# Attention stage of a hybrid decoder block: sink columns a unit ahead, background steps behind the unit's own, the gated result cast a unit later

## The chip, the cores and the metric

The kernel runs on one NeuronCore of a Trainium2 chip. The metric is the device time of one launch in microseconds (us). Lower is better.

The engines of the core are named as in the profile: PE is the matrix engine (TensorE), with PEld its loads of weights; DVE is the vector engine; ACT the scalar engine; POOL is GpSimd; SP is the engine that issues nearly all the DMAs here. A trailing q (SPq, DVEq) is the sequencer of that engine.

## The reference, cut to what matters

The block has 1024 positions of 1024 channels. It normalises the input, makes one wide projection of it, runs sliding-window attention (16 heads of 64, 4 key heads, window 128, one learned sink logit per head) beside a gated linear recurrence, gates both, projects both, merges them, projects once more and normalises.

```python
q, k, v, g_attn, xr, g_rnn, m_attn, m_rnn = jnp.split(h @ w_in[l], SPLIT_POINTS, axis=-1)
...
m = jnp.maximum(jnp.max(s, axis=-1, keepdims=True), sink)      # s: masked scores of 128 queries
p = jnp.exp(s - m)                                             #    against 256 keys
denom = jnp.sum(p, axis=-1, keepdims=True) + jnp.exp(sink - m)
o = jnp.einsum('bnkgqs,bnskd->bnqkgd', p / denom, vb)
...
y_attn = o * jax.nn.silu(g_attn)
merged = (jax.nn.sigmoid(m_attn) * (y_attn @ w_attn_proj[l])
          + jax.nn.sigmoid(m_rnn) * (y_rnn @ w_rnn_proj[l]))
x = x + gate[:, None, :] * (merged @ w_out[l])
```

Everything is float32. A large product is made of three products of a rounded part ("hi", ACT casts it) and a rest ("lo", DVE subtracts it): hi x hi, lo x hi, hi x lo.

## The kernel before

**The stages.** Up to about 575 us the kernel makes the projections (lines 200 to 850). From about 583 to 778 us it runs attention together with background matmuls. After that it projects the attention result (`ap_k`, line 1412), merges, and makes the output projection (line 1468 on) up to 964 us. The change lies wholly in the attention stage.

**A unit.** Attention is cut into 32 units of one key head group g = u // 8 and one block of 128 queries n = u % 8, four heads at once. The loop is at line 1331 and runs 35 turns, because a unit's steps lie up to three turns apart. From line 360 on the instruction order on PE, ACT, DVE, POOL and SP is the order in which the program calls them (`manual_schedule`, line 361): each engine does its instructions in that order, and an instruction that waits holds up all behind it on its engine. In turn u:

- `scores(u)` (997): 8 matmuls into the tile `s_ps`, of which there is one buffer. It also takes a tile `p` (`px`, three buffers) of 4 heads x 129 columns, and POOL copies the sink logits into column 129 (line 1012). In odd turns it issues loads of keys and queries (`load_kq`).
- `maxima_a(u)` (1017): ACT copies half of the scores into `px`. `maxima_d(u)` (1021): DVE copies the other half where the window's mask says so (1025; in units with n = 0 POOL's `affine_select` masks instead, 1028), and reduces `px`, sink column included, to the maxima (1030).
- `weights_a(u-1)` (1032): four exponentials on ACT. `weights_d(u-1)` (1038): DVE takes the reciprocal of the sums (1041) and multiplies (1042).
- `values(u-3)` (1071): 4 matmuls into `pv` (2 where n = 0), one buffer; at even units it issues loads of values (`load_v`).
- `join_a(u-3)` (1085): two ACT copies out of `pv` into `ob`. `join_d(u-3)` (1092): two DVE additions into `yq` (1099, 1100).
- `transposed(u-2)` (1045): four PE transposes of the weights into `pt`, one buffer.
- `split_a(u-2)` (1052): ACT casts `pt` to `phc`. `split_d(u-2)` (1057): DVE subtracts to `plc` (1060), and POOL masks both to `phm` and `plm` (1065; not where n = 0). `values` of the next turn needs all four.

**What runs between.** `piece()` (1325) advances a generator by one background product of 12 matmuls: for six turns the last slots of the projection (`run`, 623), after that the products of `rp_steps` (1132), tile `rp`. One turn has one piece, the 34th has two. A piece also calls small background steps: `prep_r` (1110) casts a half of a weight chunk on ACT and makes its rest on DVE (line 104, tile `wl`), in two of four turns; `finish` (1146) copies a finished accumulator on ACT (1150, tile `rp`) and stores it, once in four turns. They go through `put` (457), which calls them on the spot, so they stand in the engines' order ahead of `weights_d`, `join` and `split` of that turn. Stores are put off to `flush()` (594), after the pieces.

**The gated result.** Every second turn `a_prep(m)` (1195) handles two finished units: f1 multiplies `yq` by the gate on DVE (1202), f2 casts it on ACT (1207, tile `ah`), f3 subtracts the rest on DVE (1212 or 1217, tile `al`). f1 and f2 are called in one turn between `weights_d` and `values`, f3 at the same place one turn later.

Of the kernel before, what the change touches and what calls it, by code (L numbers as in the profile page):

```python
# [12 lines left out]
F32 = mybir.dt.float32  # L13
# [9 lines left out]
P = 128  # L23
S = 1024
D = 1024
# [24 lines left out]
def tile_hybrid_block(ctx, tc, x, pk, rows, posr, posi, invf, c_row, w_ss, w_gate, w_main, w_v,  # L50
                      w_g, w_ap, w_rp, w_out, out):
    nc = tc.nc
    V, A, G, T = nc.vector, nc.scalar, nc.gpsimd, nc.tensor
# [5 lines left out]
    def f32(ap):  # L59
        return ap.bitcast(F32)  # L60
# [41 lines left out]
    def rest(dst, src, scale=1.0):  # L102
        if scale == 1.0:
            V.tensor_tensor(out=dst[1][:], in0=src, in1=f32(dst[0][:]), op=ALU.subtract)  # L104
        else:
            V.scalar_tensor_tensor(out=dst[1][:], in0=src, scalar=scale, in1=f32(dst[0][:]),  # L106
                                   op0=ALU.mult, op1=ALU.subtract)
# [285 lines left out]
    W = {}  # L393
# [63 lines left out]
    def put(st_):  # L457
        Load.act = max(Load.act, Load.pe) + st_[1]
        Load.dve = max(Load.dve, Load.pe) + st_[2]
        st_[3]()  # L460
# [133 lines left out]
    def flush():  # L594
        while behind:
            behind.pop(0)()
# [121 lines left out]
    gq = []  # L718
# [244 lines left out]
    at = psx = None  # L963
    U = {}
# [12 lines left out]
    def load_kq(m):  # L977
        g, t0 = m // 4, (m % 4) * 256
        ks = at.tile([P, 2, 384], F32R, tag="ks", name="ks", bufs=2)
        kv = k_d.rearrange("(b a r j) t -> j (a r) b t", b=2, a=2, r=32, j=4)[g]  # L980
        lo = P if t0 == 0 else 0
        for rep in range(2):
            dma(ks[rep * 64:(rep + 1) * 64, :, lo:], kv[:, :, t0 - P + lo:t0 + 256])
        qs = at.tile([P, 4, 256], F32R, tag="qs", name="qs", bufs=2)
        dma(qs[:], q_d[g].rearrange("(a j) t -> a j t", j=4)[:, :, t0:t0 + 256])
        U["kq", m] = ks, qs

    def load_v(m):
# [5 lines left out]
        dma(vs[:, lo:, :], vs_d[g][:, n0 - 1 + lo:n0 + 1, :])  # L994
        U["v", m] = vs, dv

    def scores(u):
        g, n = u // 8, u % 8
        ks, qs = U["kq", u // 2]
        qc = slice((n % 2) * P, (n % 2 + 1) * P)  # L1000
        k0 = (n % 2) * P
        s_full = psx.tile([P, 1024], F32, tag="s", name="s_ps")
        s_ps = s_full[:].rearrange("p (j k) -> p j k", j=4)
        for j in range(4):
            o = s_ps[:, j, :] if n else s_ps[:, j, P:]
            for b in range(2):
                W["pe"] = T.matmul(o, qs[:, j, qc], ks[:, b, k0 + (0 if n else P):k0 + 256],  # L1007
                                   start=(b == 0), stop=(b == 1))
        px = at.tile([P, 4, P + 1], F32, tag="p", name="p", bufs=3)
        sm = at.tile([P, 2, 4], F32, tag="small", name="small", bufs=4)  # L1010
        gs = slice(g * 4, (g + 1) * 4)
        G.tensor_copy(px[:, :, P:P + 1], W["sink"][:, gs].unsqueeze(2))
        U["s", u] = s_ps, px, sm
        if n % 2 and u // 2 + 2 < 16:
            load_kq(u // 2 + 2)

# [40 lines left out]
    def split_d(u):  # L1057
        pt, phc = U.pop(("t", u))
        plc = at.tile([P, 4, P], F32R, tag="plc", name="plc")
        V.tensor_tensor(out=plc[:], in0=pt[:], in1=f32(phc[:]), op=ALU.subtract)  # L1060
        ms = []
        if u % 8:
            for s_, tag in ((phc, "phm"), (plc, "plm")):
                d_ = at.tile([P, 4, P], F32R, tag=tag, name=tag)
                G.affine_select(out=d_[:], in_=f32(s_[:]), pattern=[[0, 4], [1, P]],
                                compare_op=ALU.is_ge, fill=0.0, base=0,
                                channel_multiplier=-1)
                ms.append(d_)
        U["m", u] = [phc, plc], ms
# [34 lines left out]
    rp_acc, R, O = [], {}, {}  # L1104

    def load_r(e):
        src = w_rp[e] if e < KC else w_ap[e - KC]
        R[e] = [load_half(src[:, SL[i]]) for i in range(2)]

    def prep_r(e, i):  # L1110
        def f1():
            O[e, i] = slot()
            cast(O[e, i], R[e][i])
        put(("A", 0.62, 0, f1))
        put(("D", 0, 0.69, lambda: rest(O[e, i], R[e][i])))

    def load_y(c):
        if c < 2:
# [13 lines left out]
    def rp_steps():  # L1132
        h_ctx.close()
        pb_ctx.close()
        psr = pool(ctx, "psr", space=PSUM, side="right")
        rp_acc.extend(psr.tile([P, S], F32, name=f"rp{i}") for i in range(2))
        W["yp"] = pool(ctx, "ypool", bufs=12)
        W["tout"] = pool(ctx, "tout", bufs=1)
        W["hpool"] = pool(ctx, "hpool", bufs=7)

        def part(c, kc2):
            for kc in (2 * kc2, 2 * kc2 + 1):
                W["pe"] = mm_k([rp_acc[c % 2][:, t] for t in SL], (O.get((c, 0)), O.get((c, 1))),
                               kc, xh=yh, xl=yl)

        def finish(c):
            def f():
                flush()
                t = W["tout"].tile([P, S], F32, tag="rp", name="rp32")
                A.copy(t[:], rp_acc[c % 2][:])  # L1150
                store(tr_d[c], t[:])
            put(("A", 1.1, 0, f))

        seq = [(c, k) for k in range(4) for c in range(2)]
        seq += [(c, k) for c in range(2, KC) for k in range(4)]
        load_y(2)
        load_y(3)
        for i, (c, k) in enumerate(seq):
            part(c, k)
            if i in (1, 2, 3, 4):  # L1160
                load_y(i + 3)
            if i in (1, 2):
                prep_r(i - 1, 1)
            if i in (6, 10):
                finish(0 if i == 6 else 1)
            if i >= 8 and k == 1 and c > 2:
                finish(c - 1)
            if i % 4 == 2:
                load_r((i + 2) // 4 + 1)
            if i >= 4 and i % 4 < 2:  # L1170
                prep_r((i + 4) // 4, i % 4)
            yield
        finish(7)
# [21 lines left out]
    def a_prep(m):  # L1195

        g, t0 = m // 4, (m % 4) * 256
        y = U.pop(("yq", m))

        def f1():  # L1200
            gq = U.pop(("gq", m))
            V.tensor_tensor(out=y[:], in0=y[:], in1=gq, op=ALU.mult)

        def f2():
            if not AH:
                a_alloc()
            A.copy(U["ah", g][:, :, t0:t0 + 256], y[:])

        def f3():
            h = f32(U["ah", g][:, :, t0:t0 + 256])  # L1210
            if g < 3:
                V.tensor_tensor(out=U["al", g][:, :, t0:t0 + 256], in0=y[:], in1=h,
                                op=ALU.subtract)
            else:
                for a in range(2):
                    o = AL[g][a][t0 // HALF][:, t0 % HALF:t0 % HALF + 256]
                    V.tensor_tensor(out=o, in0=y[:, a, :], in1=h[:, a, :], op=ALU.subtract)

        return [[("D", 0, 0.69, f1), ("A", 0.62, 0, f2)], [("D", 0, 0.8, f3)]]


    C_GA, C_XR, C_GR, C_MA, C_MR = 10, 18, 26, 34, 42
# [102 lines left out]
    def piece():  # L1325
        nonlocal left
        left -= 1
        next(more)

    late, low, loaded = [], [], {}  # L1330
    for u in range(32 + 3):
        todo = (left - KEEP + (35 - u) // 2) // (35 - u)
        if u < 32:
            scores(u)
            maxima_a(u)
            maxima_d(u)
        if 1 <= u < 33:
            weights_a(u - 1)
        for _ in range(todo - todo // 2):
            piece()  # L1340
        flush()
        if 1 <= u < 33:
            weights_d(u - 1)
        for st_ in low:
            put(st_)
        low = []
        if "hpool" in W and late and ("gq", late[0]) in U and u >= loaded[late[0]] + 2:
            first_, low = a_prep(late.pop(0))
            if late:
                first_, low = first_ + low, []  # L1350
            for st_ in first_:
                put(st_)
        if u >= 3:
            values(u - 3)
            join_a(u - 3)
            join_d(u - 3)
        if 2 <= u < 34:
            transposed(u - 2)
            split_a(u - 2)
            split_d(u - 2)  # L1360
        for _ in range(todo // 2):
            piece()
        if u >= 3 and u % 2 == 0:
            late.append((u - 3) // 2)
        if u >= 2 and len(loaded) < 16 and len(loaded) <= (u - 2) // 2 and (
                len(loaded) - (late[0] if late else (u - 2) // 2) < 2):
            m = len(loaded)
            load_gq(m)
            loaded[m] = u
    del W["att"]  # L1370
    for st_ in low + [st_ for m in late for group in a_prep(m) for st_ in group]:
        put(st_)
    flush()
    at_ctx.close()
    psx_ctx.close()
# [8 lines left out]
    hpool, ypool = W["hpool"], W["yp"]  # L1384
# [223 lines left out]
```

## Time and profile before

| What | Value |
|---|---|
| median of 3 runs | 969.53 us (969.5 to 971.67) |
| the profiled execution's own time | 965.91 us |
| its span, first to last instruction | 963.9 us |
| busy share of the span: PE, DVE, ACT, POOL | 96%, 71%, 55%, 8% |
| granted TensorE clock, mean | 0.999 of full |
| scores of the first unit start | 582.88 us |
| scores of the last unit start | 753.31 us |
| last matmul of `values` starts | 776.72 us |

The profile is of one execution, and all times of its rows are from the span's start. Busy PE counts matmuls that overlap: a 128x512 matmul is shown with 0.39 us, but the next one starts 0.23 us later. So PE's busy share says little about how much time a stage could lose, and the starts of the same step in successive turns say more. In rows of the timeline the columns are the start, the duration, the engine, the line, the operation, out<-in, the shape, the count, and in brackets the idle time of the engine before it with what ended that.

### The profile page before, as it was taken

Reading aid. Unit: us, or ns where it says so; the run is one execution under the profiler, and the core shown is the slowest. Engines: PE = TensorE matmul, PEld = TensorE weight load, DVE = VectorE, ACT = ScalarE, POOL = GpSimd, SP = SyncE. Lnnn points to the kernel's source line nnn. Section 1 sums busy time; section 2 is a strip of 40 time slices with the busy share of each in tenths; the row PEclk is TensorE's granted clock in tenths of the full one; section 3 lists DMA queues with packets and bytes.
Section 4 is the critical chain, followed back from the end, with each engine's and each line's share of the span. In section 5 each row is a group of like instructions: output and inputs, shape, how many; then the busy total and the mean of one; then the engine's idle time right before and its main releaser. Section 6 shows DMA issues by size and latency. Waiting matters only on the chain.

```text
span 963.9 us, 12413 instructions
## 1 busy us (share of the span) xinstructions
PE 922.8 (96%) x4261; PEld 746.6 (77%) x4261; DVE 685.0 (71%) x1068; ACT 530.6 (55%) x1036; POOL 81.2 (8%) x137
## 2 busy tenths in 40 slices
PE   5899999999999999999999989989999999999997
PEld 3688687778888888888888768767777788888886
DVE  8978798767659946875796787777878736655532
ACT  7435645454567665956675776767776622212311
POOL 1055000000000000000000001123232200000000
PEclk9999999999999999999999999999999999999999
DMA  8824575751333532353233349896655285536321
GB/s 322 345 66 165 205 268 191 254 186 45 110 109 109 190 106 89 125 181 109 91 139 132 142 151 302 265 333 195 194 164 178 66 305 179 173 129 219 128 90 65
DMA packets 84275, 164.19 MB, mean 170 GB/s; under 512 B 12771, under 2 KB 33251, under 8 KB 84214
## 3 DMA queue, kind: packets, MB, share of 16 engines
q1 hardware_dynamic: 83350, 161.09, 48.9%
q0 software_dynamic: 720, 2.07, 0.6%
q8 instruction: 33, 0.54, 0.2%
q14 instruction: 28, 0.23, 0.1%
q10 hardware_dynamic: 144, 0.26, 0.1%
HBM read 114.00 MB, written 49.78 MB: 170 GB/s over the span
## 4 chain that ended last, share of the span: by engine, by line
PE 67%; DVE 7%; ACT 6%; DMA 5%; issue 4%; POOL 1%; SPq 0%; DVEq 0%; ACTq 0%; POOLq 0%
PE bk L502 36%; PE rp L165 9%; PE pmain L165 5%; PE rp L1473 5%; PE pgate L775 5%; PE pmain L1473 4%; DMA ks<-k_d 2%; PE pv L1079 1%; PE s_ps L1007 1%; DVE wl L104 1%; DMA dv<-dv_d 1%; DMA r<-w_rp 1%; ACT wh L98 1%; DVE plc L1060 1%; ACT p L1035 1%
## 5 line engine op out<-in xcount | busy, mean ns | idle before, releaser
L502 PE MATMUL bk<-nh,wl 128*128 128x512 f32 x368 | 143.9, 391 | 1.9 <-DVE wl L104 1.7
L502 PE MATMUL bk<-nl,wh 128*128 128x512 f32 x368 | 144.4, 392 | 0.0
L502 PE MATMUL bk<-nh,wh 128*128 128x512 f32 x368 | 144.4, 392 | 0.0
L104 DVE TENSOR_TENSOR wl<-r,wh 128x512 fp32r<-128x512 f32 x108 | 74.4, 693 | 18.9 <-ACT wh L98 18.8
L98 ACT CAST wh<-r 128x512 fp32r<-128x512 f32 x108 | 66.3, 618 | 37.0 <-PE pmain L165 10.0
L502 PEld LDWEIGHTS bk<-nh,wl 128*128 128x128 f32 x368 | 69.1, 188 | 18.8 <-DVE wl L104 3.0
L502 PEld LDWEIGHTS bk<-nl,wh 128*128 128x128 f32 x368 | 69.1, 188 | 15.2
L502 PEld LDWEIGHTS bk<-nh,wh 128*128 128x128 f32 x368 | 69.1, 188 | 14.3
L502 PE MATMUL bk<-hh,wl 128*128 128x512 f32 x184 | 71.9, 391 | 0.9 <-DVE wl L106 0.5
L502 PE MATMUL bk<-hl,wh 128*128 128x512 f32 x184 | 72.2, 392 | 0.0
L502 PE MATMUL bk<-hh,wh 128*128 128x512 f32 x184 | 72.2, 392 | 0.0
L104 DVE TENSOR_TENSOR wl<-ws,wh 128x512 fp32r<-128x512 f32 x80 | 54.2, 683 | 4.3 <-ACT wh L98 4.3
L98 ACT CAST wh<-ws 128x512 fp32r<-128x512 f32 x80 | 48.2, 615 | 4.0 <-DVE ws L524 2.2
L1035 ACT ACTIVATE p<-p,small 128x129 f32<-128x129 f32 x128 | 50.0, 400 | 0.0
L502 PEld LDWEIGHTS bk<-hh,wl 128*128 128x128 f32 x184 | 34.5, 188 | 9.5 <-DVE wl L104 0.9
L502 PEld LDWEIGHTS bk<-hl,wh 128*128 128x128 f32 x184 | 34.6, 188 | 7.6
L502 PE MATMUL bk<-hha,wl 128*128 128x512 f32 x92 | 36.5, 397 | 4.0 <-DVE wl L104 3.9
L502 PEld LDWEIGHTS bk<-hh,wh 128*128 128x128 f32 x184 | 34.6, 188 | 7.2
L1007 PE MATMUL s_ps<-ks,qs 128*128 128x256 f32 (+1 forms) x256 | 37.6, 289 | 0.0
L605 ACT ACTIVATE c<-bk 128x512 f32<-128x512 f32 x31 | 18.5, 596 | 33.6 <-PE bk L502 31.4
L502 PE MATMUL bk<-hha,wh 128*128 128x512 f32 x92 | 36.2, 394 | 0.0
L502 PE MATMUL bk<-hla,wh 128*128 128x512 f32 x92 | 36.1, 392 | 0.0
(339 smaller groups left out, 2184.9 us busy)
## 6 DMA issues: line engine op xcount, KB each, us to landing
r<-w_main SPq DMA_DIRECT2D x100, 256.0 KB, 4.1
wada<-w_ss SPq DMA_DIRECT2D x16, 512.0 KB, 8.4
qs<-q_d SPq DMA_DIRECT2D x16, 512.0 KB, 6.0
ks<-k_d SPq DMA_DIRECT2D x24, 192.0 KB, 4.4
xt<-x SPq DMA_DIRECT2D x8, 512.0 KB, 7.4
q_d<-rhi SPq DMA_DIRECT2D x16, 256.0 KB, 3.9
q_d<-rlo SPq DMA_DIRECT2D x16, 256.0 KB, 3.6
wg<-w_gate SPq DMA_DIRECT2D x8, 512.0 KB, 4.7
```

What stands on the lines that cost most here:

```text
L98: A.copy(dst[0][:], src)
L104: V.tensor_tensor(out=dst[1][:], in0=src, in1=f32(dst[0][:]), op=ALU.subtract)
L165: mm = T.matmul(ps[hf], ww, xx[kc][hf], start=(kc == 0 and ww is w_h and xx is xh), stop=(kc == KC - 1 and xx is xl))
L502: W["pe"] = T.matmul(ps, ww[:, c], b[kc][xx_], start=(first and kc == 0 and i == 0), stop=(kc == 3 and i == 2), skip_group_check=not first)
L605: A.activation(t["t"], s(), AF.Tanh, scale=0.5)
L775: W["pe"] = T.matmul(ps[:, SL[hf]], ww[:, c0:c0 + P], xx_[:, SL[hf]], start=(ic == 0 and i == 0), stop=(ic == 1 and i == 2))
L1007: W["pe"] = T.matmul(o, qs[:, j, qc], ks[:, b, k0 + (0 if n else P):k0 + 256], start=(b == 0), stop=(b == 1))
L1035: A.activation(px[:, j, :], px[:, j, :], AF.Exp, bias=sm[:, 0, j:j + 1], accum_out=sm[:, 1, j:j + 1])
L1060: V.tensor_tensor(out=plc[:], in0=pt[:], in1=f32(phc[:]), op=ALU.subtract)
L1079: W["pe"] = T.matmul(pv[:], b, m[:].rearrange("p j q -> p (j q)"), start=(i == 0), stop=(i == len(prods) - 1))
L1473: T.matmul(ps[:, sl], lhs[k][th][:, ts_], w[:, sl], start=(k == 0 and w is h_ and lhs is mh), stop=(k == KC - 1 and lhs is ml))
```

## The change

- A new step `sink(u)` takes the tile `px` and lets POOL write the sink column. It is called for unit u+1 in turn u, after `split` and ahead of the masks; `scores` takes the tile from there.
- The masks on POOL become a step of their own (`masks`), called behind `split_d` and `sink`.
- `prep_r` and `finish` no longer call their ACT and DVE steps on the spot: they append them to two lists, and `do_later()` calls all ACT steps, then all DVE steps, at the end of the turn. Outside the attention loop they are called at once, as before.
- `a_prep` returns its three steps. In the loop f1 is called at the end of a turn, f2 in the next turn behind `weights_a` and ahead of the pieces, f3 at the end of that turn.
- All pieces of a turn are called ahead of `values`. This differs in the one turn with two pieces.

```diff
+    def sink(u):
+        px = U["p", u] = at.tile([P, 4, P + 1], F32, tag="p", name="p", bufs=3)
+        gs = slice(u // 8 * 4, u // 8 * 4 + 4)
+        G.tensor_copy(px[:, :, P:P + 1], W["sink"][:, gs].unsqueeze(2))
+
     def scores(u):
...
-        px = at.tile([P, 4, P + 1], F32, tag="p", name="p", bufs=3)
         sm = at.tile([P, 2, 4], F32, tag="small", name="small", bufs=4)
-        gs = slice(g * 4, (g + 1) * 4)
-        G.tensor_copy(px[:, :, P:P + 1], W["sink"][:, gs].unsqueeze(2))
-        U["s", u] = s_ps, px, sm
+        U["s", u] = s_ps, U.pop(("p", u)), sm
...
         V.tensor_tensor(out=plc[:], in0=pt[:], in1=f32(phc[:]), op=ALU.subtract)
+        U["m", u] = phc, plc
+
+    def masks(u):
+        phc, plc = U["m", u]
         ms = []
...
+    later_a, later_d = [], []
+
     def prep_r(e, i):
         def f1():
             O[e, i] = slot()
             cast(O[e, i], R[e][i])
-        put(("A", 0.62, 0, f1))
-        put(("D", 0, 0.69, lambda: rest(O[e, i], R[e][i])))
+        later_a.append(f1)
+        later_d.append(lambda: rest(O[e, i], R[e][i]))
+        if "att" not in W:
+            do_later()
+
+    def do_later():
+        for todo in (later_a, later_d):
+            while todo:
+                todo.pop(0)()
...
                 A.copy(t[:], rp_acc[c % 2][:])
                 store(tr_d[c], t[:])
-            put(("A", 1.1, 0, f))
+            later_a.append(f)
+            if "att" not in W:
+                do_later()
...
-        return [[("D", 0, 0.69, f1), ("A", 0.62, 0, f2)], [("D", 0, 0.8, f3)]]
+        return f1, f2, f3
...
-    late, low, loaded = [], [], {}
+    late, high, loaded = [], [], {}
+    sink(0)
     for u in range(32 + 3):
...
         if 1 <= u < 33:
             weights_a(u - 1)
-        for _ in range(todo - todo // 2):
+        low = [steps_[2] for steps_ in high]
+        while high:
+            high.pop(0)[1]()
+        for _ in range(todo):
             piece()
         flush()
         if 1 <= u < 33:
             weights_d(u - 1)
-        for st_ in low:
-            put(st_)
-        low = []
-        if "hpool" in W and late and ("gq", late[0]) in U and u >= loaded[late[0]] + 2:
-            first_, low = a_prep(late.pop(0))
-            if late:
-                first_, low = first_ + low, []
-            for st_ in first_:
-                put(st_)
         if u >= 3:
             values(u - 3)
...
             split_d(u - 2)
-        for _ in range(todo // 2):
-            piece()
+        if u + 1 < 32:
+            sink(u + 1)
+        if 2 <= u < 34:
+            masks(u - 2)
+        if "hpool" in W:
+            for f in low:
+                f()
+            if late and ("gq", late[0]) in U and u >= loaded[late[0]] + 2:
+                high.append(a_prep(late.pop(0)))
+                high[0][0]()
+        do_later()
         if u >= 3 and u % 2 == 0:
             late.append((u - 3) // 2)
```

After the loop what is left of `high` and `late` is called in the order f1, f2, f3, as before.

More of the change, by code (lines that the diff above doesn't have):

```diff
@@ L1370, in tile_hybrid_block @@
     del W["att"]
-    for st_ in low + [st_ for m in late for group in a_prep(m) for st_ in group]:
-        put(st_)
+    for steps_ in high:
+        steps_[1]()
+        steps_[2]()
+    for m in late:
+        for f in a_prep(m):
+            f()
     flush()
```

## Prediction

> **What bounds the kernel now.** I read the page first, then the stage by windows, then the chain of waits, the sum of waits and the timeline of single turns.
>
> ```profile
> span 963.9 us, 12413 instructions
> ```
>
> ```profile
> 616.00:652.00 36.00, 31.80 (x160) 23.78 (x159) 27.25 (x51) 24.79 (x81) 8.62 (x17) 1.00 1.02 317
> 660.00:760.00 100.00, 95.35 (x491) 74.21 (x490) 80.68 (x152) 74.24 (x237) 26.44 (x52) 1.00 0.49 155
> ```
>
> The columns of the windows are the stretch, its length, busy time of PE, PEld, DVE, ACT and POOL with their counts, the granted clock, the DMA share and GB/s. The attention stage has two halves. Up to 652 us the DMA engines are full (share 1.02). After 660 us they are half idle (0.49), DVE is busy for 81% and PE looks full at 95%, which for overlapping matmuls does not say that it lost nothing. The chain of waits has the same border:
>
> ```profile
> 620.15 8.64 DMA ks<-k_d
> 628.86 8.47 DMA r<-w_rp
> 637.34 8.70 DMA dv<-dv_d
> ...
> 697.60 0.95 PE s_ps L1007 x8
> 698.55 2.76 PE rp L165 x12
> 701.31 0.93 PE pv L1079 x4
> 702.25 0.44 PE pt L1049 x4
> ```
>
> From 620 to 646 us the end of one load starts the next. No order of ACT and DVE steps makes that shorter. The last four rows are one turn in which PE waits for nothing: 0.95 + 2.76 + 0.93 + 0.44 = 5.08 us. That is the least a turn can take. Now the turns as they are (start of scores, and for the turns without scores the first matmul of the piece):
>
> ```profile
> 652.33 1.19 PE L1007 MATMUL s_ps<-ks,qs 128*128 128x256 f32 x8
> ...
> 753.31 1.19 PE L1007 MATMUL s_ps<-ks,qs 128*128 128x256 f32 x8
> ...
> 758.98 0.71 PE L165 MATMUL rp<-yh,wh 128*128 128x512 f32 x2
> ...
> 765.59 0.71 PE L165 MATMUL rp<-yh,wh 128*128 128x512 f32 x2
> ```
>
> Turns 13 to 30 are 18 turns in 753.31 - 652.33 = 100.98 us. In two of them (units 16 and 24) `values` has 2 matmuls instead of 4, which makes 5.08 - 0.46 = 4.62. So the least is 16 x 5.08 + 2 x 4.62 = 90.5, and 10.5 us are lost. Turn 31 takes 758.98 - 753.31 = 5.67, lost 0.6. Turn 32 has no scores, least 5.08 - 0.95 = 4.13; it takes 765.59 - 758.98 = 6.61, lost 2.5. Together **13.6 us** that PE loses after the DMA half. The waits (window 652 to 776 us) and one bad turn show to what:
>
> ```profile
> ACT ah L1207 <- DVE yq L1202: 28.8, 11, 3.7
> DVE yq L1099 <- ACT ob L1089: 16.4, 11, 2.0
> PEld pv L1079 <- ACT phc L1054: 7.8, 7, 2.0
> ```
>
> ```profile
> 689.04 0.99 ACT L1150 COPY rp<-rp 128x1024 f32<-128x1024 f32 x1
> 690.25 1.20 PE L1007 MATMUL s_ps<-ks,qs 128*128 128x256 f32 x8
> 690.72 0.68 DVE L104 TENSOR_TENSOR wl<-r,wh 128x512 fp32r<-128x512 f32 x1
> 691.32 0.17 DVE L1041 RECIPROCAL small<-small 128x4 f32<-128x4 f32 x1
> 691.53 0.69 DVE L1042 TENSOR_TENSOR p<-p,small 128x512 f32<-128x512 f32 x1
> 692.14 0.69 DVE L1202 TENSOR_TENSOR yq<-yq,r 128x512 f32<-128x512 f32 x1
> 692.86 0.62 ACT L1207 CAST ah<-yq 128x512 fp32r<-128x512 f32 x1 [2.30 <-DVE yq L1202]
> 693.49 0.37 ACT L1088 COPY ob<-pv 64x256 f32<-64x256 f32 x1
> 694.25 0.59 ACT L1054 CAST phc<-pt 128x512 fp32r<-128x512 f32 x1
> 694.26 0.42 DVE L1099 TENSOR_TENSOR yq<-pv,ob 64x256 f32<-64x256 f32 x1 [1.44 <-ACT ob L1089]
> 694.69 0.43 DVE L1100 TENSOR_TENSOR yq<-pv,ob 64x256 f32<-64x256 f32 x1
> 694.74 0.59 ACT L1019 COPY p<-s_ps 128x512 f32<-128x512 f32 x1
> 695.15 0.69 DVE L1060 TENSOR_TENSOR plc<-pt,phc 128x512 fp32r<-128x512 f32 x1
> 695.22 0.42 ACT L1035 ACTIVATE p<-p,small 128x129 f32<-128x129 f32 x1
> 695.22 0.46 PE L1079 MATMUL pv<-phc,vs 128*128 128x512 f32 x1 [1.01 <-ACT phc L1054]
> 695.76 0.74 DVE L1025 COPY_PREDICATED p<-mgt,s_ps 128x512 f32<-128x512 uint32 x1
> 695.97 0.64 POOL L1065 TENSOR_SCALAR_AFFINE_SELECT plm<-plc 128x512 fp32r<-128x512 f32 x1 [0.36 <-DVE plc L1060]
> 696.39 0.39 ACT L1035 ACTIVATE p<-p,small 128x129 f32<-128x129 f32 x1
> 696.78 0.69 DVE L1030 TENSOR_REDUCE small<-p 128x4 f32<-128x516 f32 x1 [0.28 <-POOL p L1012]
> 697.36 1.19 PE L1007 MATMUL s_ps<-ks,qs 128*128 128x256 f32 x8
> ```
>
> This turn takes 697.36 - 690.25 = 7.11 us. ACT and DVE wait for each other in turn. ACT's `ah` cast stands ahead of `ob` and `phc` and waits 2.30 us for DVE's f1, which stands behind `wl`, the reciprocal and the multiplication. Then DVE idles 1.44 us for `ob`, and PE idles for `phc`. So the bound after 652 us is a loop of DVE and ACT, not PE. DVE's steps from start to start: `wl` 0.60, reciprocal 0.21, multiplication 0.61, f1 0.61, idle 1.44 or a little more, additions 0.43 + 0.46, `plc` 0.61, masked copy 0.74, idle 0.28, reduction 0.61: some 6.6 us against PE's 5.08.
>
> **The change part by part.**
>
> *The `ah` cast a turn later.* f1 runs at the end of a turn, f2 in the next turn behind the exponentials, over a microsecond after f1 ends. So ACT's 2.30 and DVE's 1.44 go. Without the two idles and without f1 or `wl` ahead of it, the loop is only DVE's own work: 0.21 + 0.61 + 0.43 + 0.46 + 0.61 + 0.74 + 0.61 = 3.67, plus one of f1 and f3 (0.61) each turn = 4.28, plus `wl` (0.60) in two of four turns = 4.88; mean 4.58. That is under 5.08, so PE's own 5.08 becomes the bound.
>
> *Background behind the unit's own.* I check the chain in a turn without stalls, time 0 at its scores. `values` ends at 0.95 + 2.76 + 0.93 = 4.64, the last matmul 0.16 later (0.39 shown, 0.23 apart): 4.8. The two `ob` take 694.25 - 693.49 = 0.76: 5.55. `phc` to 6.14. DVE adds from 5.55 to 6.44, `plc` to 7.13, POOL's `plm` starts 0.13 later (695.97 against 695.84) and ends at 7.9. PE wants `plm` for the fourth matmul of the next `values`, at 5.08 + 3.71 + 0.69 = 9.48. That is 1.6 us to spare, where now it is short. What is moved goes behind `plc`: f1 or f3 to 7.66, `wl` to 8.26. Who now waits for it is the masked copy of the next unit: it runs to 9.0, the reduction to 9.6, reciprocal and multiplication to 10.4, and the next additions are due at 5.55 + 5.08 = 10.63. The masked copy frees the only `s_ps`, which PE wants at 10.16: 1.1 to spare. ACT: `phc` to 6.14, a cast of weights 0.62, copy of scores 0.59, exponentials 696.78 - 695.22 = 1.56, `ah` 0.62, to 9.5; the next `ob` is due at 9.88. Once in four turns `finish` (0.99) comes in too, and ACT is then 0.6 late for `ob`; the 1.6 cover it. I leave 0.6 in all for the five or so turns where this comes together with `ah`. The weights so prepared are for products three turns later, so half a turn of delay costs nothing. `finish` reads an accumulator that is overwritten three pieces on: nothing either.
>
> *Sink a unit ahead.* It now waits on POOL for the transposes of the same turn (`px` has three buffers), at about 5.3, ahead of `phm`, which can start only after `phc` at 6.14; the copy is short enough for that gap. Queued behind it are only the masks. It saves DVE the 0.28 ahead of the reduction. These lie in the same loop and in the 13.6, not beside it. If the gap were gone, each mask would come 0.2 later, inside the 1.6.
>
> *Stores and loads on SP.* `finish` a half turn later means its store is flushed a turn later. Before, SP stood at it:
>
> ```profile
> SPq L57 <- ACT rp L1150: 42.9, 8, 13.7
> ```
>
> The loads of values behind it now go first. At a DMA share of 0.49 that is worth nothing to PE. In the DMA half no `finish` has come yet, and the bytes ahead of `dv` are the same, so 646 us stays.
>
> *Two pieces in one turn* ahead of `values`: in the next turn one piece then covers the chain to `plm`. As computed, that suffices: nothing.
>
> Where the port between DVE and POOL comes in, there is one row of each:
>
> ```profile
> 630.06 1.07 POOL L1065 TENSOR_SCALAR_AFFINE_SELECT phm<-phc 128x512 fp32r<-128x512 f32 x1 [1.56 <-ACT phc L1054]
> ...
> 630.55 1.12 DVE L1212 TENSOR_TENSOR al<-yq,ah 128x512 fp32r<-128x512 f32 x1
> ```
>
> A mask that takes 0.64 takes 1.07 here, and f3, which takes 0.69 like f1, takes 1.12, while they overlap: 0.43 for each. After the change f1 or f3 starts right behind `plc`, when `plm` starts too, so this meeting becomes the rule. If POOL loses, `plm` ends at 8.4 or, behind `wl` as well, 9.1: still in time. I take that end (DVE starts 0.1 to 0.2 earlier); the other end is the first rival. The Trainium skill, "SBUF — State Buffer", section "Who interferes with whom", says that a DVE instruction with two SBUF inputs and a GpSimd instruction that reads SBUF share a read port, and that the one that starts second waits for the whole of the other. By that rule f1, f3 and `wl` (two SBUF inputs) meet the masks, while the additions and `plc` (one input in PSUM) don't; the two rows agree with it.
>
> **The sum.** 13.6 lost, less 0.6 that stays, is a gain of 13.0 us. The profiled execution, 965.91 with a span of 963.9, becomes 952.9. It is 3.6 below the median of the runs shown, 969.53; from that median the forecast is **956.5**.
>
> **The rivals.**
>
> 1. *DVE becomes the bound by the port.* If in each turn two DVE instructions wait 0.43 for the two masks, DVE's mean is 4.58 + 0.86 = 5.44, 0.36 over PE, and over 20 turns 7 us come back: gain 6, **963.5**. For it: the two rows. Against: `phm` (from 6.2) mostly runs beside additions and `plc`, of which no row here shows such a delay, and at one wait per turn the mean is 5.01, still under PE.
>
> 2. *The DMA half shrinks too.* PE is idle there for 36 - 31.80 = 4.2 us. If loads are called earlier because PE comes earlier, up to that is won on top: **952.3**. For it: the bytes are the same and 317 GB/s is not the highest rate of the trace. Against: share 1.02 and a chain that is all DMA. The same page, section "A bandwidth-pool intuition that's wrong", lists about 358 GB/s from HBM to one core; an estimate by that figure is 36 x (1 - 317/358) = 4.1 us.
>
> 3. *Slower: scores wait for `s_ps`.* The masked copy stands behind f1, f3 and `wl` now, and scores of the next turn wait for it. It decides from 1.1 us of DVE delay in a turn on. Were DVE late by another 0.9 in each of 20 turns, 18 us would be lost instead of the 13.6: **974**. Against: DVE would need 4.88 + 2.0 in every turn, and no row gives that.
>
> 4. *Nothing arrives at the end.* The order does what it says, but the next stage starts on loads that come no earlier: about **969.5**. Against: these loads hang on buffers that attention frees.
>
> **How the numbers follow.** Forecast 0.54, rival 1 0.20, rival 2 0.12, rival 3 0.07, rival 4 0.07. The range from 951 to 964 holds the first three, 0.86 together; without either of the outer two it would hold too little. About 0.3% (2.9 us) is what a measurement of this kernel can tell from no change. Faster by more: 0.86. Within: 0.07. Slower by more: 0.07.
>
> **What would show it.** Right: the waits of `ah` for f1 and of the additions for `ob` nearly gone; turns 13 to 32 at 5.1 us; the reduction no longer waiting for the sink copy; `plm` often at about 1.0 us; the chain in that stretch mostly PE; turn 11 still waiting for `dv`. Wrong: turns at 5.4 with a chain of DVE (rival 1); PE waiting at scores for the masked copy (rival 3); early turns shorter too (rival 2); attention shorter but a gap after it (rival 4).

## The result, and the profile after

The changed kernel takes 953.12 us (median of 4 runs, 951.39 to 953.65) beside 969.51 us for the kernel before on the same chip (968.31 to 971.67). The ratio is 0.9825 with a 95% interval of 0.9804 to 0.9847: faster by 16.4 us. The forecast was 956.5, the range 951 to 964.

The profiled execution of after is its longest of the four, 953.65 us; that of before, 965.91, lies below all the others of before in the table. So the two traces differ by only 12.3 us, which is not the 16.4 of the medians; the end of this section says what is known of the rest. First the head of the page of after, with the shares of its chain by engine:

```profile
span 951.6 us, 12442 instructions
...
PE 915.3 (96%) x4261; PEld 748.7 (79%) x4261; DVE 689.2 (72%) x1068; ACT 529.3 (56%) x1036; POOL 91.5 (10%) x137
...
PE 63%; DMA 11%; DVE 8%; ACT 5%; issue 3%; SPq 1%; POOL 0%; DVEq 0%; ACTq 0%
```

Now the timeline of PE, with the start of the scores of the first unit, of unit 13 and of unit 31, and the first matmuls of the pieces of turns 32 and 33:

```profile
583.74 1.00 PE L1012 MATMUL s_ps<-ks,qs 128*128 128x128 f32 x8
...
652.75 1.19 PE L1012 MATMUL s_ps<-ks,qs 128*128 128x256 f32 x8
...
743.19 1.19 PE L1012 MATMUL s_ps<-ks,qs 128*128 128x256 f32 x8
...
748.27 0.70 PE L165 MATMUL rp<-yh,wh 128*128 128x512 f32 x2
...
752.74 0.70 PE L165 MATMUL rp<-yh,wh 128*128 128x512 f32 x2
```

Turns 13 to 30 take 743.19 - 652.75 = 90.44 us where they took 100.98, and the prediction had worked out 90.5 as the least. Turn 31 takes 5.08, its least, instead of 5.67, and turn 32 takes 4.47 instead of 6.61. That is 10.54 + 0.59 + 2.14 = 13.3 us, and the forecast was 13.0 of 13.6. Turns 0 to 12 take 652.75 - 583.74 = 69.01; before had 69.45 (from 582.88 to 652.33). The stage starts 0.9 us later and the end stage takes 0.5 longer, which together with the 0.4 of the first half leaves the 12.3 of the two traces.

The chain of waits names PE alone from 646.62 to 743 us. Its rows, from the last loads on:

```profile
629.45 7.47 DMA r<-w_rp
636.94 9.54 DMA dv<-dv_d
646.62 0.70 PE pv L1085 x2
...
673.26 0.95 PE s_ps L1012 x8
674.21 2.76 PE rp L165 x12
676.98 0.93 PE pv L1085 x4
677.91 0.44 PE pt L1051 x4
```

This is the clean turn of 5.08, now in every full turn of this stretch. The sum of waits from 652 to 764 us (the waiting engine and line, who ends the wait, us in total, times, longest):

```profile
POOL p L1000 <- PE pt L1051: 29.2, 17, 2.2
...
ACT ob L1094 <- PE pv L1085: 14.0, 11, 5.1
...
DVE yq L1105 <- ACT ob L1095: 8.2, 10, 3.8
...
ACT ah L1224 <- DVE yq L1219: 1.1, 1, 1.1
...
PEld pv L1085 <- POOL plm L1071: 0.5, 1, 0.5
```

The wait of the cast `ah` for f1 is down from 28.8 to 1.1 us. PE hardly waits for anybody. ACT now waits for PE's values: the order has turned round, and PE leads. The additions still wait 8.2 us for `ob`. That costs nothing, since DVE has come to the end of its work when it waits. The sink copy waits 29.2 us on POOL and nobody waits for it.

**The part of 16.4 that the two traces don't show.** The time of the kernel before goes with the granted clock of the run: over 46 of its runs in this study the median is 966.56 at 0.999 (6 runs), 967.97 at 0.997 and 0.998 (13 runs) and 969.4 at 0.995 and less (22 runs). Its first profile was one at 0.999. Two runs of after, at 0.996 and 0.999, do not show that order (951.39 and 953.65). What a lower mean stands for in a trace is in the last section. At 0.997 and 0.998, where both kernels have runs, before has a median of 967.97 and after, over its two sets, 952.93 (6 runs): 15.0 us apart. The 13.3 of turns 13 to 32 are nearly the whole of it. A second trace of each kernel (below) differs by 18.1 us of span, 967.8 to 949.7: 13.4 in turns 13 to 32, 2.8 in turns 0 to 12, 1.8 ahead of attention and 0.1 behind turn 32. So the two pairs agree on turns 13 to 32 and in no other stretch.

### The profile page after: what moved, and what is told of

Read it like the earlier page. It is cut to its first block, busy times and chain, and to the rows that moved or that the text cites. A ratio compares the mean times of both kernels' runs of the same rounds, so it can differ in the third digit from the quotient of the medians.

```text
span 951.6 us, 12442 instructions
## 1 busy us (share of the span) xinstructions
PE 915.3 (96%) x4261; PEld 748.7 (79%) x4261; DVE 689.2 (72%) x1068; ACT 529.3 (56%) x1036; POOL 91.5 (10%) x137
## 4 chain that ended last, share of the span: by engine, by line
PE 63%; DMA 11%; DVE 8%; ACT 5%; issue 3%; SPq 1%; POOL 0%; DVEq 0%; ACTq 0%
PE bk L502 36%; PE rp L165 9%; PE pgate L775 5%; PE rp L1498 3%; PE pmain L1498 3%; DMA wo<-w_out 3%; PE pv L1085 2%; PE s_ps L1012 2%; DMA ks<-k_d 2%; PE pmain L165 1%; DMA tt<-tr_d 1%; PE pt L1051 1%; DMA dv<-dv_d 1%; DMA smr<-smr_d 1%; DMA r<-w_rp 1%
## 5 line engine op out<-in xcount | busy, mean ns | idle before, releaser
L104 DVE TENSOR_TENSOR wl<-r,wh 128x512 fp32r<-128x512 f32 x108 | 79.3, 737 | 16.3 <-ACT wh L98 16.3
```

## The experiments

The expectations name the theories by letters. A is the theory of the prediction: the loop of ACT's cast `ah` and DVE's steps was the loss of turns 13 to 32, and the cast a turn later breaks it. The rivals hold that another part of the change carries the gain, or that DVE's load and the one `s_ps` tile set the turn. For each run stand its median and its ratio to the kernel before on the same chip, with the 95% interval in brackets. Turns 13 to 30 are measured each time from the start of the scores of unit 13 to those of unit 31.

### One part alone: the cast

The kernel before, with f2 a turn later; f1 and f3 stay ahead of `values`, and the background steps stay where they were.

```diff
+        low = [steps_[2] for steps_ in high]
+        while high:
+            high.pop(0)[1]()
         for _ in range(todo - todo // 2):
             piece()
...
-        for st_ in low:
-            put(st_)
+        for f in low:
+            f()
...
+            high.append(a_prep(late.pop(0)))
+            high[0][0]()
```

> The kernel before with one part of the change alone: the cast f2 of the gated result a turn later, f1 and f3 at their old place. Theory A (the bound is the loop in which ACT's ah cast waits for DVE's f1 and DVE's additions then wait for ACT's ob): both idles go, DVE's own work with the 0.28 us wait for the sink copy is 4.86 us a turn in the mean, under PE's 5.08, so most of the 16 us comes: 956 to 960 us against 969.5 before. Rival B (what counts is that background steps no longer stand ahead of plc): a small gain, 963 to 968 us.

It takes 955.6 us (954.15 to 956.39), ratio 0.9859 [0.9843, 0.9875] to 968.69, 0.4 us below the range of A. From the timeline of PE:

```profile
651.69 1.19 PE L1007 MATMUL s_ps<-ks,qs 128*128 128x256 f32 x8
...
742.62 1.20 PE L1007 MATMUL s_ps<-ks,qs 128*128 128x256 f32 x8
```

Turns 13 to 30: 90.93 us, half a microsecond above after. From its sum of waits, 652 to 764 us:

```profile
DVE small L1030 <- POOL p L1012: 3.4, 15, 0.3
...
DVE yq L1099 <- ACT ob L1089: 3.1, 4, 2.0
```

No wait of `ah` for f1 is left among its rows. The reduction still waits for the sink copy, 15 times by 0.2 us; that and all else in which this kernel differs from after cost the half microsecond together. So the cast alone does nearly the whole work of this stretch. Its median lies 2.5 above the 953.12 of after, measured on another chip. The traces show 0.8 of that in turns 13 to 32 (90.93 + 5.09 + 4.78 beside 90.44 + 5.08 + 4.47); the rest I have not located, and the two intervals touch.

### One part alone: the background behind

The kernel before, with the casts of weights and `finish` collected and called at the end of the turn, and all pieces ahead of `values`.

```diff
-        put(("A", 0.62, 0, f1))
-        put(("D", 0, 0.69, lambda: rest(O[e, i], R[e][i])))
+        later_a.append(f1)
+        later_d.append(lambda: rest(O[e, i], R[e][i]))
...
-        for _ in range(todo - todo // 2):
+        for _ in range(todo):
             piece()
...
-        for _ in range(todo // 2):
-            piece()
+        do_later()
```

> The kernel before with the weight casts, their rests and the accumulator copies alone put to the end of the turn. Theory A: DVE's loop has the same members in another order, still about 6.6 us in a turn with f1, so 967 to 970 us. Rival B: PE's wait for plc and plm goes, 956 to 962 us.

It takes 965.95 us (964.82 to 966.12), ratio 0.9968 [0.9956, 0.9979]. It has 101.14 us in turns 13 to 30, beside 100.98 in before: nothing is won there. The sum of waits, 652 to 764 us, has the old loop in full:

```profile
ACT ah L1218 <- DVE yq L1213: 26.7, 10, 2.9
DVE yq L1099 <- ACT ob L1089: 14.4, 10, 1.4
```

The median is 2.7 us below that of before, a little more than A allowed. The traces do not show where it comes from. Turns 31 and 32 take 5.09 and 5.96 us instead of 5.67 and 6.61, and turns 0 to 12 take 68.30 instead of 69.45, which is no more than this half varies between runs (below). But the stage starts 0.7 later and what follows turn 32 takes 1.5 longer than in the first trace of before, and the two spans are equal (963.9).

### One part alone: the sink a unit ahead

The kernel before, with the sink copy of unit u + 1 and the masks at the end of the steps of turn u.

```diff
+            sink(u + 1)
+        if 2 <= u < 34:
+            masks(u - 2)
         for _ in range(todo // 2):
             piece()
```

> The kernel before with the sink copy a unit ahead alone. Theory A: DVE is the bound after 652 us, so 0.28 us of its idle time in each of some 20 turns is worth up to 5 us: 964 to 968 us, and no wait of the reduction for the sink copy. Rival C (the reduction is off the path, its wait worth nothing): 969 to 970 us.

It takes 965.49 us (964.42 to 966.97), ratio 0.996 [0.9947, 0.9974]: within what was expected. Turns 13 to 30 take 98.95 us, 2.0 less, and the reduction's wait for the sink copy is gone. On the old order, where DVE is a part of the loop, this wait of 0.28 counts; without it `ah` still waits 25.1 us. Once the cast is moved, it hardly counts: the first experiment has 90.93 with the wait, after has 90.44 without.

### After, without the later cast

The changed kernel with f2 in the turn of f1, right behind it.

```diff
-        while high:
-            high.pop(0)[1]()
+        high.clear()
...
                 high[0][0]()
+                high[0][1]()
```

> The changed kernel, but f2 in the same turn right behind f1, both at the end of the turn. Theory A: ACT again waits for f1, about 1.5 us in every second turn, but now ahead of the next copy of scores and not ahead of ob and phc; there is 1.6 us to spare to plm, so little is lost: 953 to 958 us. Rival D (the wait of ACT itself is the loss, wherever it stands): 963 to 968 us.

It takes 962.33 us (961.21 to 966.69), ratio 0.9939 [0.9918, 0.996]. A had 953 to 958 and is missed, though A holds that the cast matters; the time lies 0.7 below the range of rival D, for which ACT's wait is a loss wherever it stands. Turns 13 to 30 take 98.72. The reason is in one turn of its timeline (the bracket is the idle time before the instruction and who ended it):

```profile
692.09 1.21 PE L1012 MATMUL s_ps<-ks,qs 128*128 128x256 f32 x8 [0.15 <-DVE p L1027]
...
695.76 0.62 ACT L1224 CAST ah<-yq 128x512 fp32r<-128x512 f32 x1 [2.69 <-DVE yq L1219]
696.29 1.01 ACT L1165 COPY rp<-rp 128x1024 f32<-128x1024 f32 x1
...
697.71 0.59 ACT L1021 COPY p<-s_ps 128x512 f32<-128x512 f32 x1
...
698.45 0.72 DVE L1027 COPY_PREDICATED p<-mgt,s_ps 128x512 f32<-128x512 uint32 x1
...
699.23 1.22 PE L1012 MATMUL s_ps<-ks,qs 128*128 128x256 f32 x8 [1.79 <-DVE p L1027]
```

The cast waits 2.69 us for f1. Behind it on ACT stand `finish`, a cast of weights and then the copy of the scores, which starts at 697.71, 4.4 us after the scores have ended (692.09 + 1.21). DVE's masked copy comes behind it and frees `s_ps` only then. PE idles 1.79 us, and the turn takes 699.23 - 692.09 = 7.14. This is the place of the prediction's third rival (scores wait for `s_ps`), reached by a late ACT and not by a late DVE. So this order needs the later cast too: it is worth 98.72 - 90.44 = 8.3 us of turns 13 to 30 here and 10.1 on the old order, where the loss was at `ob` and `phc`.

### Is the first trace of before a fair base?

The kernel before once more, unchanged.

> The kernel before once more, unchanged, for a second profile of it. Its first profile has 965.9 us, below all its other times (968 to 971.7), and the two profiles differ by 12.3 us where the medians differ by 16.4. If the first profile was a lucky execution, this one is at 968 to 970 and a stretch of turns is longer in it; if profiles of it are always shorter, it is at 966 again.

968.76 us (967.3 to 970.25, 10 runs), ratio 1.0006 [0.9995, 1.0017]. Its profiled execution took 969.85 at a clock of 0.995, with 69.47 us in turns 0 to 12 and 100.89 in turns 13 to 30. So the attention stretch is the same as in the first trace, within 0.1. The 3.9 us between the two traces of before lie ahead of attention (2.3) and behind turn 30 (1.6); the last section shows what most of them are. What the prediction read from the attention rows holds for both traces; what it took as the span was some 3 us below the usual.

### How much has DVE to spare?

The changed kernel with the reduction to the maxima done twice, 0.61 us of DVE a turn by the prediction's count.

```diff
-        V.tensor_reduce(out=sm[:, 0, :], in_=px[:], axis=AX.X, op=ALU.max, negate=True)
+        for _ in range(2):
+            V.tensor_reduce(out=sm[:, 0, :], in_=px[:], axis=AX.X, op=ALU.max, negate=True)
```

> The changed kernel with the reduction to the maxima done twice, 0.61 us more of DVE in each turn. Theory A (DVE is the next bound, with about 0.43 us idle in a turn): 0.2 to 0.3 us more in each of some 20 turns, 957 to 960 us. Rival E (PE leads by far, DVE has over 0.6 us to spare): 952 to 954 us.

It takes 964.94 us (964.55 to 967.17), ratio 0.9968 [0.9953, 0.9983]. The direction is A's; the size is missed by 5 us. Turns 13 to 30 take 98.34, 7.9 more than in after, or 0.44 a turn. So DVE had less to spare than was thought. The timeline of DVE in after shows how much, from one masked copy to the next:

```profile
676.22 0.76 DVE L1027 COPY_PREDICATED p<-mgt,s_ps 128x512 f32<-128x512 uint32 x1
677.08 0.69 DVE L1032 TENSOR_REDUCE small<-p 128x4 f32<-128x516 f32 x1
...
678.76 0.42 DVE L1105 TENSOR_TENSOR yq<-pv,ob 64x256 f32<-64x256 f32 x1 [0.18 <-ACT ob L1095]
...
680.86 0.75 DVE L1027 COPY_PREDICATED p<-mgt,s_ps 128x512 f32<-128x512 uint32 x1
...
683.86 0.42 DVE L1105 TENSOR_TENSOR yq<-pv,ob 64x256 f32<-64x256 f32 x1 [0.64 <-ACT ob L1095]
...
685.96 0.68 DVE L104 TENSOR_TENSOR wl<-r,wh 128x512 fp32r<-128x512 f32 x1
686.56 0.73 DVE L1027 COPY_PREDICATED p<-mgt,s_ps 128x512 f32<-128x512 uint32 x1
...
690.91 1.12 DVE L104 TENSOR_TENSOR wl<-r,wh 128x512 fp32r<-128x512 f32 x1
691.95 0.74 DVE L1027 COPY_PREDICATED p<-mgt,s_ps 128x512 f32<-128x512 uint32 x1
```

A turn without `wl` is 680.86 - 676.22 - 0.18 = 4.46 us of DVE. One with `wl` is 686.56 - 680.86 - 0.64 = 5.06, and one with a `wl` that meets a mask is 691.95 - 686.56 = 5.39. Two of each four turns have no `wl`: the mean is (2 x 4.46 + 5.06 + 5.39) / 4 = 4.84. The prediction had 4.58. The masked copy takes 0.86 until the next instruction starts (677.08 - 676.22), not 0.74, and `wl` 1.04 where it meets a mask of POOL, as seven of the ten between 650 and 750 us do. To spare are 5.08 - 4.84 = 0.24. These four turns are examples, and a turn whose unit has no masked copy is shorter. Counted over eight turns, up to the masked copy at 716.37 us, DVE idles for 1.99 of 40.15 us, which is 0.25 a turn. From the timeline of the run with two reductions:

```profile
692.54 1.42 DVE L1033 TENSOR_REDUCE small<-p 128x4 f32<-128x516 f32 x2
```

The second reduction adds 1.42 - 0.69 = 0.73. By that 0.73 - 0.24 = 0.49 a turn would be lost; 0.44 were. PE then waits in two places, and longer for `plm`, which comes late with `plc`, than for `s_ps`. From the sum of waits, 652 to 764 us:

```profile
PEld pv L1086 <- POOL plm L1072: 7.4, 14, 0.8
...
PEld s_ps L1012 <- DVE p L1027: 2.9, 6, 0.5
```

### What bounds the first half?

The changed kernel without the loads of the rest part `yl` in chunks 2 to 7 (3.1 MB less); the hi part is multiplied in its place, so the rest part is missing from these products.

```diff
-        l_ = W["yp"].tile([P, S], F32R, tag="Y", name="yl")
+        l_ = h_
...
-        dma(l_[:], yl_d[c])
```

> The changed kernel without the loads of the lo part of the recurrence's result for chunks 2 to 7 (3.1 MB less; the hi part is multiplied in its place). Theory A (the turns up to 12 are bound by DMA): of the 7.7 us that turns 4 to 12 lose, 5 to 7 go, 946 to 948 us. Rival F (they are held by DVE and ACT after the end of the projection): 951 to 953 us.

It takes 946.33 us (945.2 to 947.61), ratio 0.9774 [0.9755, 0.9792]. The timeline of PE has unit 0 and unit 13 at

```profile
582.60 1.00 PE L1012 MATMUL s_ps<-ks,qs 128*128 128x128 f32 x8
...
645.03 1.20 PE L1012 MATMUL s_ps<-ks,qs 128*128 128x256 f32 x8
```

which is 62.43 us for turns 0 to 12 where after had 69.01, and 90.46 for turns 13 to 30. So the first half is bound by its bytes, and I see no order of ACT and DVE steps that would win these 6.6 us (4.2 beside the second trace of after, below). The windows of after and of this kernel say the same (stretch, length, busy time of PE, PEld, DVE, ACT and POOL, granted clock, DMA share, GB/s):

```profile
616.00:652.00 36.00, 30.32 (x159) 24.11 (x158) 28.36 (x50) 24.71 (x81) 11.15 (x17) 1.00 1.02 320
```

```profile
616.00:645.00 29.00, 28.64 (x156) 24.05 (x155) 27.73 (x50) 23.70 (x79) 10.93 (x16) 1.00 1.04 308
```

In both the DMA share is above 1. With fewer bytes PE is busy for 28.64 of 29 us; in after it idles 5.7 of 36.

### Loads in another order, twice

The changed kernel with the values loaded at the head of the turn ahead of their use, and the third weights loaded and prepared later.

```diff
-        if n % 2 == 0 and u // 2 + 1 < 16:
-            load_v(u // 2 + 1)
...
-            if i % 4 == 2:
-                load_r((i + 2) // 4 + 1)
-            if i >= 4 and i % 4 < 2:
+            if i % 4 == (0 if i == 4 else 2) and i not in (2,):
+                load_r(2 if i == 4 else (i + 2) // 4 + 1)
+            if i in (6, 7):
+                prep_r(2, i - 6)
+            if i >= 8 and i % 4 < 2:
                 prep_r((i + 4) // 4, i % 4)
...
+        if u >= 3 and u % 2 and (u - 3) // 2 + 1 < 16:
+            load_v((u - 3) // 2 + 1)
```

> The changed kernel with loads in the order in which they are due: values' operands at the head of a turn, the first weight chunk in the DMA half (512 KB) two pieces later, behind the last yl. Theory A: the wait for dv in turn 11 (2.4 us) goes and a part of it comes back at yl, as only 512 KB leave the full stretch: 950.5 to 952.5 us. Rival G (the same bytes, the same time): 953 us.

It takes 950.7 us (949.8 to 952.85), ratio 0.9826 [0.9804, 0.9847], with 65.10 us in turns 0 to 12 and no wait for `dv` in turn 11. It was run once more, on one chip with the changed kernel:

> The changed kernel once more, on the same chip as the next two, to compare with them, and for a second profile of it: 952 to 954 us; turns 13 to 30 again at 90.4 us, since PE bounds them.

> The changed kernel with loads in the order in which they are due, beside the changed kernel on one chip. Theory A, after the first run of it: 1.5 to 4 us faster than that, the turns up to 12 shorter by 3 to 4 us. Rival G (the same bytes, the same time; the first run was chance): within 1 us of it.

The changed kernel has 952.72 (951.69 to 953.01), ratio 0.9837 [0.9816, 0.9857] to 967.33. The new order of loads has 951.89 (949.17 to 952.04), ratio 0.9828 [0.9808, 0.9848]. In the traces turns 0 to 12 take 66.67 us in after and 64.32 in the new order. The rate of the DMA engines does not tell the orders apart: from 616 to 652 us it is 331 GB/s in the new order, 320 and 338 in the two traces of after. And the difference in time, 0.8 us, is within the two intervals, where rival G had it, and below the 1.5 to 4 of A. So the first half is shorter in both traces, and whether the kernel is faster stays open. The two traces of after show by how much this half varies by itself: 69.01 and 66.67. Turns 13 to 30 are 90.44 and 90.47.

### After, without the background behind

The changed kernel with the casts of weights and `finish` back at their old place.

```diff
-        later_a.append(f1)
-        later_d.append(lambda: rest(O[e, i], R[e][i]))
+        put(("A", 0.62, 0, f1))
+        put(("D", 0, 0.69, lambda: rest(O[e, i], R[e][i])))
...
-            later_a.append(f)
+            put(("A", 1.1, 0, f))
```

> The changed kernel, but with the casts and rests of weights and the accumulator copies at their old place inside the pieces (f1 and f3 still at the end of the turn). Theory A, in which the later cast carries the gain: within 2 us of the changed kernel. Rival B (the background's place carries a part of it): 3 us or more slower.

953.0 us (951.68 to 954.1), ratio 0.9841 [0.9819, 0.9863], 0.3 from the changed kernel on the same chip, with 90.45 us in turns 13 to 30. As A expected: on top of the later cast, the place of the background steps carries nothing that can be measured.

## Why the prediction was right, point by point

**The bound and the least.** Right. The loop of the cast and DVE's steps was what made turns of 6 to 7 us, and with it broken PE's own 5.08 became the bound. 90.44 stand where 90.5 were worked out. The 0.6 kept back for turns with `finish` was not needed in that stretch. What is left is 0.3 in turn 32.

**Which part of the change does it.** The prediction gave the gain to one loop and put the three parts into it. That was right for the sum and too coarse for the parts. The cast alone gives 10.1 of the 10.5 us of turns 13 to 30 (100.98 to 90.93). The background's place gives nothing there, and the sink gives 2.0 alone and next to nothing once the cast is moved. That the sink's 0.28 "lie in the same loop and in the 13.6, not beside it" is what the runs show.

**The margins.** This is the step that was off. The text had 1.1 us to spare where the scores wait for `s_ps`, and 0.50 of DVE a turn (5.08 - 4.58). In the tight turn above the masked copy ends at 691.95 + 0.74 = 692.69 and the next scores start on the timeline of PE at

```profile
692.89 1.20 PE L1012 MATMUL s_ps<-ks,qs 128*128 128x256 f32 x8
```

so 0.2 are left there, and of DVE's mean 0.24. Three things eat them: `wl` at 1.04 beside a mask, the masked copy at 0.86, and a start of the additions that DVE itself makes late in the turn behind one with `wl`. The additions were taken to be ready at PE's time in every turn. So the delay from which on rival 3 (slower) costs time is 0.24 and not 1.1. 0.73 us of DVE a turn cost 7.9 us, more of it at `plm`, where the text had 1.6 to spare, than at `s_ps`; a cast that waits on ACT costs 8.3, mostly at `s_ps`. Neither makes the kernel slower than before. The forecast held because what was left of the margins was enough, not because they were as wide as the text had them.

**The port (rival 1).** It was expected that f1 or f3 meets `plm` in each turn, with POOL as the loser, or else with DVE. The groups of POOL's masks of the rest, before (583 to 775 us) and after (583 to 765), and of `wl` from 650 to 750 us, before and after (count, then total and mean ns of one, then idle before and who ended it):

```profile
L1065 POOL TENSOR_SCALAR_AFFINE_SELECT plm<-plc 128x512 fp32r<-128x512 f32 x28 | 18.6, 664 | 20.0 <-DVE plc L1060 20.0
```

```profile
L1071 POOL TENSOR_SCALAR_AFFINE_SELECT plm<-plc 128x512 fp32r<-128x512 f32 x28 | 27.4, 977 | 14.0 <-DVE plc L1062 14.0
```

```profile
L104 DVE TENSOR_TENSOR wl<-r,wh 128x512 fp32r<-128x512 f32 x8 | 5.5, 688 | 0.0
```

```profile
L104 DVE TENSOR_TENSOR wl<-r,wh 128x512 fp32r<-128x512 f32 x10 | 9.9, 988 | 0.0
```

The mask loses 0.31 us and is still in time; f1 and f3 lose nothing in the median (0.68 in after). `wl`, which starts while the mask runs, loses 0.30, and it comes in half the turns: 0.15 a turn, not the 0.86 of rival 1. So the end that the prediction took was right, and the meeting moved on by one instruction. The rule of the Trainium skill, "SBUF — State Buffer", section "Who interferes with whom", names the pair rightly. What each loses is most of what is left of the other when it starts. In the turn of the 1.12 above the timeline has

```profile
690.31 0.68 DVE L1219 TENSOR_TENSOR yq<-yq,r 128x512 f32<-128x512 f32 x1
...
690.52 0.96 POOL L1071 TENSOR_SCALAR_AFFINE_SELECT plm<-plc 128x512 fp32r<-128x512 f32 x1 [0.70 <-DVE plc L1062]
```

The mask starts 0.39 us before f1 makes way for `wl` (690.91), and takes 0.32 more than its 0.64. `wl` starts 0.57 before the mask ends (691.48), and takes 0.44 more than its 0.68. That fits a wait for the other's end to about 0.1 us, and one mask can so lose to f1 and make `wl` lose in turn. The prediction read its own two rows as one meeting of f3 and the mask; in the trace the mask of 630.06 had met the multiplication that started at 629.95, which has two SBUF inputs too, and f3 then met the mask.

**The first half (rival 2).** It did not shrink in the profiled pair (69.45 to 69.01), and it is 66.67 in the second trace of after. The run without `yl` shows that the bytes bound it, and the change leaves the bytes as they are. That this half varies by 2.3 us between two traces of one kernel was not foreseen. Whether a part of the shorter one comes from the change, as rival 2 has it, two traces of each kernel (69.45 and 69.47 before) do not settle.

**The end of the stage (rival 4).** The gain arrives. What follows turn 32 takes 198.9 us instead of 198.3, and 199.6 in the second trace of after; the second trace of before has 199.7, of which 1.3 belong to a stretch at half clock (last section). So the end is 0.5 to 1.3 us longer. For a part of that PE comes to a product whose weights `wo` have not been split yet, a wait that neither trace of before has. From the waits of PE from 764 us on:

```profile
PEld rp L1498 <- DVE wo L1434: 0.5, 1, 0.5
```

Rival 4 thus has a small part of its way: 0.5 to 1.3 of 13 us.

**The size.** The forecast 956.5 is 3.4 above the median measured, and the 952.3 of rival 2 is nearer to it by number, though rival 2's sign, shorter early turns, is plain in only one of the two traces of after. The term of the sum that can be read from the traces came out at 13.3 instead of 13.0. The rest of the 16.4 lies outside turns 13 to 32. Between runs of like clock 15.0 remain, and the variation of the first half can hold the 1.7 that is then left. This last step is argued, not shown.

## What to carry to other kernels

Where two engines that execute in order wait for each other in turn, look for the instruction whose operand is made latest, with something urgent queued behind it: moving that one cast by a turn was worth 13.1 us of median (968.69 to 955.6), and the place of the background steps around it nothing that could be measured. Work out the least a turn can take from a turn without stalls, but take the margins from the turn with the most work in it, and count a delayed start of the engine itself along with its instructions. And compare a gain with the trace stretch by stretch: turns 13 to 30 agreed within 0.1 us between runs of one kernel, while the whole execution moved by 2 to 4.

## What was not expected of the hardware

The kernel before has a spread of its own with the granted clock: 966.05 to 968.02 us at 0.999 and 967.3 to 971.66 at 0.993 to 0.995, though in the windows from 583 to 752 us the clock reads 1.00 in both of its traces. The 3.9 us between its two profiled executions (0.999 and 0.995) lie outside turns 0 to 30 altogether. Most of them are two short stretches of the trace at 0.995, at 122 to 126 and at 767 to 771 us, in which the clock reads 0.50 and matmuls start 0.43 us apart instead of 0.23. The window from 123 to 125 us, and two rows of PE's timeline in it:

```profile
123.00:125.00 2.00, 2.00 (x7) 1.51 (x6) 1.90 (x8) 1.05 (x3) 0.00 (x0) 0.50 0.00 0
```

```profile
123.26 0.63 PE L502 MATMUL bk<-hha,wh 128*128 128x512 f32 x1
123.68 0.63 PE L502 MATMUL bk<-hha,wl 128*128 128x512 f32 x1
```

Each stretch costs about 1.6 us: 8 starts take 3.37 us (122.45 to 125.82) instead of 1.83, and from the transposes of turn 32 to the next `values` it is 4.78 instead of the 3.21 of the first trace. The trace at 0.999 has no such stretch, nor have those of after up to 940 us. So here the lower clock makes the time longer, and not the other way round. Seven such stretches are in the traces of this study, each within 1.7 us behind an idle of PE of 1.45 to 2.44 us (2.14 and 1.57 us for these two). But after idles for 2.14 us at the first place too and keeps its clock, so what starts them stays open. Two of the seven lie behind the idle of turn 32, which the change removes. That may be a part of the 1.4 us by which the 16.4 of the medians exceed the 15.0 at like clock; no run tests it.

And with full DMA engines the rate is not one number, not even for one kernel. From 616 to 652 us the first trace of after moved 320 GB/s at a share of 1.02, and the second

```profile
616.00:652.00 36.00, 32.45 (x176) 26.50 (x175) 30.45 (x56) 26.43 (x84) 11.33 (x19) 1.00 1.01 338
```

In the same window, with a share above 1, the first trace of before moved 317 GB/s and the new order of loads 331; without `yl` it was 308 up to 645 us.
